# A hybrid decoder step on one core: the order of keys, queries, tables and sample work in the GLA heads, and of the couples' combinations

## The chip, the cores and the metric

One core of one Trainium2 chip. The metric is the device time of one execution in microseconds (us), the median of several runs. The kernel before ran three times: 1547.67 us median, 1545.2 to 1551.61.

## What is computed

One layer for a prompt of 2048 tokens and for eight single sample tokens, all float32, with a model width of 1024:

```python
ada = jax.nn.silu(c) @ w_ada + b_ada
shift, scale, gate = jnp.split(ada, 3, axis=-1)
hn = _rmsnorm(x, g_norm) * (1.0 + scale[:, None]) + shift[:, None]
z = hn @ w_in
xa, za, q, k, v, glr, zg = jnp.split(z, SPLITS, axis=-1)
...
log_alpha = jax.nn.log_sigmoid((glr @ w_gla_g2 + b_gla_g2).astype(f32)) / GLA_TAU
...
o, S_new = _gla_chunked(qh, kh, vh, log_alpha, S0.astype(f32))
o = o * lax.rsqrt(jnp.mean(o * o, axis=-1, keepdims=True) + EPS) * g_gla_norm.astype(f32)
y_gla = o.reshape(Bn, T, D_GLA).astype(x.dtype) * jax.nn.silu(zg)
mix = jnp.concatenate([y_lru, y_gla], axis=-1) @ w_out
x = x + gate[:, None] * mix
```

The first two columns of z, 1024 each, feed an RG-LRU group (convolution, gates, a real-gated recurrence, y_lru); the rest a gated linear attention (GLA) of four heads with keys of 128 and values of 256, whose decay comes from a product of rank 16 and a log-sigmoid. A last RMSNorm ends it.

## The kernel before

**Stages.** The prompt is worked in two halves of 1024 tokens. The stages follow one another on TensorE (PE): the adaLN vectors and the first head (0 to 90 us of the profile), the GLA heads of half 0 (to 366), the "couples" of half 0 (to 645; the RG-LRU's blocks and the columns of zg, each a 2x2 block product by seven products of a Strassen kind), the heads of half 1 (to 976), the couples of half 1 (to 1195), the output projection (to 1551). Every float32 operand of a product is split into a high and a low part, and each product is three products of these parts; splitting is a copy on ScalarE (ACT) and a subtraction on VectorE (DVE).

**Order.** ACT, DVE, GpSimd (POOL), the DMA queue of SyncE (SP) and PE each run their instructions strictly in the order in which they were written or scheduled, so a late instruction holds all that stand behind it. The order is written by a list of work that is due: `after(units, fn)` puts a piece of work into it, and `tick` lets it out when so many units of product work have been written. A unit is 24 products of 512 columns. `in_order`, `behind` and `issue_after` fix an engine's order where the scheduler might change it.

**A GLA head** (`gla_head`, L1107 and on) writes the value projection (`values`, eight tiles of 128 tokens, evicted at L893/894), and then for each segment s of 512 tokens: the decay (`decay`: product L913, ACT's L918, L920 exponential and L921 logarithm, DVE's L919 and L922; `gla_decay`: four scans L935, L944 exponential, L945, and L947/948 exponentials), the key projection (`project`, L683 to L685, 24 products; combined with the decay at L956) and the query projection (combined at L960). The chunks of the segment follow as due work: `gla_start` (scores L985, turned keys L988, their masks and splits L989 to L995), `gla_chunk` (L1011 to L1024, the state S at L1020), `gla_norm` (L1032), and one unit later `gla_turn`, which turns the normalized output on PE (L1080) for L1146 or, in the last head, for the gate at L1153. Exponential and logarithm are reached in ACT by loading a table set ahead of each use (the ACT_TABLE_LOAD rows of L920/921, L944 and L972); `silu` (L1084) uses a tanh. In half 1 the states of the sample tokens (`sample_state`, L795 to L809, L1043 to L1052) are worked between.

**Weights.** In half 0 weights are loaded raw (L332), split (L338 ACT, L339 DVE) and stored in DRAM (L365, `parts`); in half 1 they are loaded back (L341). `sample_cols` (products L302, copy L303, L308, L310) multiplies the eight sample tokens by the raw weight columns while they are there; in the first couples these products use the tiles called gps.

**Between the heads and the couples of half 0** `second_rows` normalizes the second 1024 rows of x (L242), turns them (L253) and adds them up on POOL for the Strassen operands; `sums` makes S1 to S4. `load_op` (L1202) brings S3 and S4 back by SP's queue and `split_op` (L1209/1210) splits them. `Couple.prepare` (L1359 to L1396) splits a couple's four weight blocks (L1368 ACT, L1369 DVE), runs the sample columns and combines the blocks on POOL (L1384 to L1386); T2 is the block that needs L1385. `acc` tiles, of which there are four banks of PSUM, take the products of projections, values, decays and couples; `tp` tiles (two banks) take turned tiles.

Of the kernel before, what the change touches and what calls it, by code (L numbers as in the profile page):

```python
# [37 lines left out]
CTS = (0, 8)  # L38
B11, T2, T1, B21, T3, B22, T4 = range(7)
# [13 lines left out]
def hybrid_kernel(ctx, tc, i, o):  # L53
# [243 lines left out]
    def sample_cols(raw, n, dst, tmp, bank, units=0.5):  # L297

        ps = bank()
        for r in range(2):  # L300
            for g in range(4):
                PE.matmul(ps[32 * g:32 * g + 32, :n], fs[:, 4 * r + g], raw(4 * r + g), start=r == 0, stop=r == 1)  # L302
        S.copy(tmp[:, :n], ps[:, :n])  # L303

        def turn():
            po = bank()
            for a in range(n // P):
                PE.matmul(po[:, a * NS:(a + 1) * NS], tmp[:, a * P:(a + 1) * P], sel4, start=True, stop=True)  # L308
            for a, (d, scale) in enumerate(dst):
                V.tensor_scalar(d, po[:, a * NS:(a + 1) * NS], scale, None, op0=OP.mult)  # L310
        after(units, turn)
# [42 lines left out]
    def raw_rows(col, n, k0=0, nk=KT):  # L354
        raw = wp.tile([P, 1088], F32, tag="wr", name="wr")[:, :nk * n].rearrange("p (k n) -> p k n", n=n)
        SP.dma_start(raw, i["w_in"][0, k0 * P:(k0 + nk) * P, col:col + n].rearrange("(k p) n -> p k n", p=P))
        return raw

# [228 lines left out]
    def first_head():  # L587
# [71 lines left out]
        with tc.issue_after(last[V.engine]), tc.issue_after(last[S.engine]):  # L659
            normalize(st, [xsr], NS, "junk")  # L660
# [248 lines left out]

    def decay(h, c0, n):  # L910
# [9 lines left out]
        S.activation(e, e, AF.Exp, scale=-1.0)  # L920
# [136 lines left out]
    def sample_out(h, b0, st, s0, done, more):  # L1057
# [13 lines left out]
        rsqrt(gp, rs[:, :1], ss[:, :1], 1, P, 1.0 / DV)  # L1071
        V.tensor_scalar(os_, os_, rs[:, :1], None, op0=OP.mult)
# [10 lines left out]
    def silu(z, src):  # L1083
        S.activation(z, src, AF.Tanh, scale=0.5)  # L1084
        V.scalar_tensor_tensor(z, z, 1.0, src, op0=OP.add, op1=OP.mult)
# [21 lines left out]
    def gla_head(half, h, k, wv=None, w=None):  # L1107
        final = k == 3
        if wv:
            wk, wq = wkq0  # L1110
            v, prep0, rest = first_head()
        else:
            v = values(half, h, w or value_weights(h))
            own = own_samples(half, h)
            wk = weights(K0 + h * DK, DK, samples=own)
            wq = weights(Q0 + h * DK, DK, samples=own)
            if own:
                after(1, lambda: sample_qk(h, 1, wk))
                after(2, lambda: sample_qk(h, 0, wq))
# [3 lines left out]
        def chunks(s, c):  # L1123
# [13 lines left out]
            after(1, lambda: finish(s), True)  # L1137
# [31 lines left out]
        for s in range(2):  # L1169
            if wv and s == 0:  # L1170
                prep[s] = prep0
                pk = project(wk, 512, 512)
                rest()
            else:
                prep[s] = gla_qk(h, s, wq, wk, dec, pk)
                pk = None
            if s == 0:
                dec = gla_decay(half, h, 1)
                after(0, lambda: chunks(0, 0), True)
            tick(0.5)  # L1180
        if half == 1 and k == 0:
            sample_heads(0)
        if wv:
            modulate_samples(st, xsr)
            with tc.issue_after(last[V.engine]), tc.issue_after(last[S.engine]):
                constants()
        if final:
            wz = [weights(ZG + (2 * h + dt) * P, P) for dt in range(2)]
            z = [gp.tile([P, 2, 512], F32, tag=tag, name="z", bufs=2) for tag in ("vh", "vl")]
            for dt in range(2):  # L1190
                for s in range(2):
# [5 lines left out]
                    tick(0.5)  # L1197

# [13 lines left out]
    def second_rows(sc, then):  # L1212
# [8 lines left out]
        def norm(p, x):  # L1221
            normalize(xp, x)
            after(0.5, lambda: step(p, x, 0))

        def step(p, x, k):
# [14 lines left out]
            elif p < 3:  # L1240
                after(0.5, lambda: load(p + 1))
            else:
                after(1.5, then)
# [12 lines left out]
    def sums(pool, then):  # L1256
# [20 lines left out]
        def other(k, s2):  # L1277
# [9 lines left out]
            after(*((1, lambda: one(k + 1)) if k < 3 else (1.5, then)))  # L1287
# [40 lines left out]
    class Couple:  # L1328
# [30 lines left out]
        def prepare(self, q):  # L1359
# [13 lines left out]
            if q == B11:  # L1373
                self.slot(q)
                split(q, b11)
                if self.half == 0:
                    tmp = am.rearrange("p c t -> p (c t)")
                    if turns[3]:
                        turns[3] = 0
                        tmp = lp.tile([P, 512 + 4], F32, tag="xa", name="tmp")  # L1380
# [4 lines left out]
                G.tensor_tensor(t, b22, b11, op=OP.subtract)  # L1385
                G.tensor_tensor(b12, b22, b12, op=OP.subtract)  # L1386
# [11 lines left out]
        keep = None  # L1398
# [262 lines left out]
    def couples(cs, lead=5, at={}):  # L1661

        n = len(cs)
        for k in (1, 2):
            cs[-k].turn = k
        uses = [(0, 0), (0, 1)]
# [9 lines left out]
        def prepare(u):  # L1676
            if u < len(uses):
# [3 lines left out]
                cs[m].prepare(q)  # L1681

        cs[0].load_raw()
        for u in range(lead):
            prepare(u)
# [12 lines left out]

    for k, h in enumerate(HEADS):
        gla_head(0, h, k, wv0 if k == 0 else None)  # L1700
# [32 lines left out]
    def samples_silu():  # L1733
        with behind(V), behind(S):
# [5 lines left out]
    scs.append(Scratch(3))  # L1740
    for k, h in enumerate(HEADS):
        gla_head(1, h, k, w=w if k == 0 else None)
# [543 lines left out]
```

## Time and profile before

| | |
|---|---|
| median of three runs | 1547.67 us |
| the profiled execution | 1552.06 us |
| its span in the profile | 1550.3 us |
| mean granted clock of PE | 0.971 |
| instructions | 22539 |

The profile is one execution. The page's first part gives each engine's busy time and share of the span. The windows give, for a stretch of time, its length and each engine's busy time with its count of instructions, then PE's granted clock (1.00 is full speed), the DMA engines' busy share and GB/s. The waits of an engine are its idle times, grouped by the instruction that waited and by the one that ended last before it could start ("PE tp L1080 <- DVE on L1032: 18.8, 5, 6.3" reads: PE's line 1080, which writes the tile tp, waited five times, 18.8 us in all and 6.3 us at most, and DVE's line 1032, which wrote the tile on, had ended last). The timeline has the start, the length, engine, line, operation, tiles out and in, sizes and count. In groups by line stand the count, busy time and the mean of one in ns, and after the bar the idle time before them. PE's products overlap, so a mean of 390 ns for 512 columns is longer than the distance between two starts.

### The profile page before, as it was taken

Reading aid. Unit: us, or ns where it says so; the run is one execution under the profiler, and the core shown is the slowest. Engines: PE = TensorE matmul, PEld = TensorE weight load, DVE = VectorE, ACT = ScalarE, POOL = GpSimd, SP = SyncE. Lnnn points to the kernel's source line nnn. Section 1 sums busy time; section 2 is a strip of 40 time slices with the busy share of each in tenths; the row PEclk is TensorE's granted clock in tenths of the full one; section 3 lists DMA queues with packets and bytes.
Section 4 is the critical chain, followed back from the end, with each engine's and each line's share of the span. In section 5 each row is a group of like instructions: output and inputs, shape, how many; then the busy total and the mean of one; then the engine's idle time right before and its main releaser. Section 6 shows DMA issues by size and latency. Waiting matters only on the chain.

```text
span 1550.3 us, 22539 instructions
## 1 busy us (share of the span) xinstructions
PE 1437.3 (93%) x8113; PEld 1185.5 (76%) x8113; DVE 1112.8 (72%) x2283; ACT 760.3 (49%) x1367; POOL 292.9 (19%) x285
## 2 busy tenths in 40 slices
PE   8979889899899999988887999999999699999997
PEld 6868778787677777878776788788888587778886
DVE  5775666466587888758786765576798597678886
ACT  4534445644665766444635351466775342144332
POOL 1450521224212222054253300000112000000000
PEclk9989999999999999999998999999999899999999
DMA  9625446646738644977866642876617848694452
GB/s 324 240 82 184 163 147 197 219 150 219 263 131 304 220 156 134 313 252 250 293 229 222 210 163 79 312 222 192 191 54 236 330 172 305 233 346 144 151 167 109
DMA packets 204293, 321.97 MB, mean 208 GB/s; under 512 B 11730, under 2 KB 145522, under 8 KB 200461
## 3 DMA queue, kind: packets, MB, share of 16 engines
q1 hardware_dynamic: 160133, 293.00, 55.4%
q10 hardware_dynamic: 43728, 26.48, 5.4%
q8 instruction: 64, 1.05, 0.3%
q0 software_dynamic: 320, 1.05, 0.2%
q14 instruction: 48, 0.39, 0.1%
HBM read 196.86 MB, written 123.68 MB: 207 GB/s over the span
## 4 chain that ended last, share of the span: by engine, by line
PE 55%; DVE 20%; DMA 11%; ACT 8%; issue 4%; POOL 1%; SPq 0%; ACTq 0%; DVEq 0%; POOLq 0%
PE acc L1914 11%; PE tp L1914 8%; PE acc L1415 8%; PE tp L1415 6%; PE acc L685 2%; PE acc L684 2%; PE acc L683 2%; PE acc L375 2%; PE acc L377 2%; PE acc L376 2%; DVE xb L935 2%; DMA mixd<-zs 1%; DVE tg L1556 1%; DVE op L1369 1%; PE po L1019 1%
## 5 line engine op out<-in xcount | busy, mean ns | idle before, releaser
L1415 PE MATMUL acc<-op,op 128*128 128x512 f32 x1056 | 252.5, 393 | 4.9 <-DVE op L1369 2.2
L1415 PEld LDWEIGHTS acc<-op,op 128*128 128x128 f32 x1056 | 199.8, 190 | 49.1 <-DVE op L1369 3.4
L1415 PE MATMUL tp<-op,op 128*128 128x512 f32 x792 | 199.2, 396 | 2.2 <-DVE acc L1425 2.1
L1914 PE MATMUL acc<-w,a 128*128 128x512 f32 (+1 forms) x792 | 187.9, 390 | 11.9 <-ACT a L1765 7.9
L1914 PEld LDWEIGHTS acc<-w,a 128*128 128x128 f32 x792 | 147.7, 190 | 47.7 <-ACT a L1765 8.8
L1415 PEld LDWEIGHTS tp<-op,op 128*128 128x128 f32 x792 | 147.6, 189 | 37.5 <-issue 4.1
L375 PE MATMUL acc<-w,op 128*128 128x256 f32 (+1 forms) x508 | 151.7, 299 | 1.0 <-DVE xb L960 1.0
L377 PE MATMUL acc<-w,op 128*128 128x256 f32 (+1 forms) x508 | 145.5, 286 | 1.5 <-DVE op L269 1.5
L376 PE MATMUL acc<-w,op 128*128 128x256 f32 (+1 forms) x508 | 144.9, 285 | 0.0
L1914 PE MATMUL tp<-w,a 128*128 128x512 f32 x564 | 136.0, 391 | 0.0
L683 PE MATMUL acc<-op,w 128*128 128x512 f32 x296 | 124.8, 422 | 3.0 <-DMA w<-parts 3.0
L1914 PEld LDWEIGHTS tp<-w,a 128*128 128x128 f32 x564 | 105.3, 188 | 26.8 <-issue 5.2
L684 PE MATMUL acc<-op,w 128*128 128x512 f32 x296 | 118.7, 401 | 0.0
L685 PE MATMUL acc<-op,w 128*128 128x512 f32 x296 | 118.6, 401 | 0.0
L375 PEld LDWEIGHTS acc<-w,op 128*128 128x128 f32 x508 | 97.9, 193 | 3.4 <-DVE xb L960 1.3
L377 PEld LDWEIGHTS acc<-w,op 128*128 128x128 f32 x508 | 97.7, 192 | 2.0 <-DVE op L269 1.9
L376 PEld LDWEIGHTS acc<-w,op 128*128 128x128 f32 x508 | 97.5, 192 | 0.7
L1384 POOL TENSOR_TENSOR raw<-raw 128x512 f32<-128x512 f32 x14 | 24.4, 1746 | 316.6 <-DVE op L1369 267.6
L1765 ACT CAST a<-s 128x512 fp32r<-128x512 f32 x61 | 36.4, 619 | 97.1 <-issue 34.3
L1523 DVE SCALAR_TENSOR_TENSOR cv<-xa,vecT,cv 128x512 f32<-128x512 f32 x96 | 73.3, 764 | 8.0 <-ACT cv L1521 6.9
L226 ACT ACTIVATE junk<-on 128x256 bf16<-128x256 f32 x64 | 26.6, 415 | 104.3 <-DVE on L1024 92.1
L683 PEld LDWEIGHTS acc<-op,w 128*128 128x128 f32 x296 | 57.0, 192 | 15.5 <-DMA w<-parts 3.7
(413 smaller groups left out, 2985.4 us busy)
## 6 DMA issues: line engine op xcount, KB each, us to landing
wtd<-op SPq DMA_DIRECT2D x56, 512.0 KB
op<-wtd SPq DMA_DIRECT2D x56, 512.0 KB
w<-parts SPq DMA_DIRECT2D x16, 1024.0 KB
a<-mixd SPq DMA_DIRECT2D x63, 256.0 KB
parts<-w SPq DMA_DIRECT2D x15, 1024.0 KB
mixd<-zs ACTq DMA_DIRECT2D x52, 256.0 KB
wd<-scratch SPq DMA_DIRECT2D x48, 256.0 KB
w<-wd SPq DMA_DIRECT2D x10, 1024.0 KB
```

The costliest lines, as they stand in the source:

```text
L226: S.activation(junk[:m, :n], x, AF.Square, accum_out=out)
L375: PE.matmul(ps, part(0, kt, c), hi[:, kt % 4], start=kt == 0, stop=False)
L376: PE.matmul(ps, part(0, kt, c), lo[:, kt % 4], start=False, stop=False)
L377: PE.matmul(ps, part(1, kt, c), hi[:, kt % 4], start=False, stop=kt == KT - 1)
L683: PE.matmul(ps[:, :n], hi[:, kt], a, start=kt == 0, stop=False)
L684: PE.matmul(ps[:, :n], hi[:, kt], b, start=False, stop=False)
L685: PE.matmul(ps[:, :n], lo[:, kt], a, start=False, stop=kt == KT - 1)
L935: V.tensor_tensor_scan(b3[:, c], b3[:, c], b3[:, c], 0.0, op0=OP.add, op1=OP.bypass)
L1415: PE.matmul(ps, w[:, u, k], t[:, v, k], start=q < 3 and (k, u, v) == (0, 0, 0), stop=(k, u) == (3, 1), skip_group_check=True)
L1523: V.scalar_tensor_tensor(cv, xa[:, k:k + 512], cw[k], cv, op0=OP.mult, op1=OP.add)
L1765: S.copy(t[:, 0, k], (low(t) if src is None else src)[:, k])
L1914: PE.matmul(ps, t[:, u, k], w[:, v, k, c], start=(q < 3 or ps is own) and (k, u, v) == (0, 0, 0), stop=(k, u) == (3, 1), skip_group_check= ...
```

## The change

It moves work, and hardly adds or removes any. By the built programs, PE, DVE and POOL run as many products and operations as before, SP's queue as many DMAs, and ACT 36 instructions fewer, all of them table loads on balance.

- In heads that aren't the first, the two key projections come first and then the two query projections (K0, K1, Q0, Q1; in the last head of each half K0, Q0, K1, Q1 as before), and the second segment's decay product is written right after the first key projection.
- A single table set that holds exponential and logarithm is loaded once by hand (`tables`), and again only after a tanh has needed the other one.
- Chunk work starts one unit after the keys and queries are ready (was: at once); turned outputs come two units after the norm (was one; only the last segment of the last head keeps one).
- Weights of the next head's values, of keys and of queries are loaded and split at written-out units (`ahead`, `take`), one head ahead for the values; the store follows half a unit later.
- Norm and scale of the second rows are split into two pieces; `sums` goes on half a unit earlier; in the couples the sample columns and POOL's combinations come 0.75 unit later (0.5 behind a zg couple), in steps of the same size; the samples' output scale and the norm of the first samples come later.

```diff
-    def sample_cols(raw, n, dst, tmp, bank, units=0.5):
+    def sample_cols(raw, n, dst, tmp, bank, units=1):
...
+    def take(col, n, k0, nk, raw):
...
+        if raw is None:
+            SP.dma_start(both[:, :, c].bitcast(F32), parts[col, k0])
+        else:
+            with behind(S), behind(V):
+                S.copy(hi, raw)
+                V.tensor_tensor(lo, raw, hi.bitcast(F32), op=OP.subtract)
...
+            after(0.5, lambda: SP.dma_start(parts[col, k0], both[:, :, c].bitcast(F32)))
...
+        if log_exp[0]:
+            return
+        log_exp[0] = True
+        with behind(S):
+            S.add_instruction(mybir.InstLoadActFuncSet(
+                name=nc.get_next_instruction_name(), engine=S.engine, act_func_set_id=LOG_EXP))
...
-            after(1, lambda: finish(s), True)
+            after(1 if final and s else 2, lambda: finish(s), True)
...
+            V.tensor_tensor(e2, pk, e2, op=OP.mult)
+            tick(0.5)
+            b = decay(h, *SEGS[1])
+            if not final:
+                pk = project(wk, *SEGS[1])
+                tick(0.5)
+            pq = project(got[1], *SEGS[0])
+            V.scalar_tensor_tensor(e1, pq, DK ** -0.5, e1, op0=OP.mult, op1=OP.mult)
+            prep[0] = e1, e2, f
+            after(1, lambda: chunks(0, 0), True)
+            tick(0.5)
+            if final:
+                pk = project(wk, *SEGS[1])
+                tick(0.5)
+            pq = project(got[1], *SEGS[1])
+            e1, e2, f = gla_decay(half, h, 1, b=b)
+            V.tensor_tensor(e2, pk, e2, op=OP.mult)
+            V.scalar_tensor_tensor(e1, pq, DK ** -0.5, e1, op0=OP.mult, op1=OP.mult)
...
         def norm(p, x):
-            normalize(xp, x)
-            after(0.5, lambda: step(p, x, 0))
+            with behind(S):
+                ss = squares(xp, x)
+            after(0.5, lambda: scale(p, x, ss))
...
+                times(x, scales(xp, ss, 2))
+            after(1, lambda: step(p, x, 0))
...
-            after(*((1, lambda: one(k + 1)) if k < 3 else (1.5, then)))
+            after(*((0.5, lambda: one(k + 1)) if k < 3 else (1.5, then)))
...
-                if self.half == 0:
...
-                    sample_cols(lambda kt: r[:, kt].rearrange("p b n -> p (b n)"), 2 * P,
-                                [(zsam[:, n], 1.0) for n in self.sam], tmp, gps)
-                t = self.t2 = lp.tile([P, 4, P], F32, tag="t2", name="t2")
-                G.tensor_tensor(b11, b12, b11, op=OP.subtract)
...
+                (self.combine if now else lambda: after(self.wait, self.combine))()
...
+        keep, wait = None, 0.75
```

Three places in the built order show what moves. Lines on the left are those of each kernel. The first is ACT in half 1, in the second head, where keys and queries are made. Before (e and xb are the decay's tiles, f its chunk ends, scratch the samples' states, smp the samples' decay):

```order
L920 ACTIVATE e<-e 128x512
L921 ACT_TABLE_LOAD
L921 ACTIVATE e<-e 128x512
L795 CAST scratch<-scratch 128x256
L944 ACT_TABLE_LOAD
L944 ACTIVATE f<-f 128x5
L947 ACTIVATE e<-xb 128x512
L918 ACTIVATE e<-acc,vecT 128x8
L948 ACTIVATE xb<-xb 128x512
L920 ACTIVATE e<-e 128x8
L921 ACT_TABLE_LOAD
L921 ACTIVATE e<-e 128x8
```

And now (ob is a turned output of the head before, L1222):

```order
L951 ACTIVATE e<-e 128x512
L952 ACTIVATE e<-e 128x512
L813 CAST scratch<-scratch 128x256
L975 ACTIVATE f<-f 128x5
L813 CAST scratch<-scratch 128x256
L978 ACTIVATE e<-xb 128x512
L947 ACTIVATE e<-acc,vecT 128x8
L979 ACTIVATE xb<-xb 128x512
L951 ACTIVATE e<-e 128x8
L952 ACTIVATE e<-e 128x8
L1222 ACTIVATE ob<-tp,gsc 128x512
L1003 ACTIVATE smp<-xb 128x8
```

The exponential (now L951) and logarithm (L952) stand without a load between them, as do L975, L978 and L979, and the turned output of the head before has come in among them.

The second is PE in the same head, from the second decay's product to the scores. Before (op and w are the operands of the projection, tp<-xb,e the scores, acc<-gls,g2s the decay):

```order
L913 MATMUL acc<-gls,g2s 128x512
L683 MATMUL acc<-op_6279,w 128x512
L684 MATMUL acc<-op_6279,w 128x512
L685 MATMUL acc<-op_6279,w 128x512
L683 MATMUL acc<-op_6279,w 128x512
L985 MATMUL tp<-xb,e 128x128 x4
L988 MATMUL tp<-ident,e 128x128 x4
```

And now, where the scores are L1016:

```order
L701 MATMUL acc<-op_6280,w 128x512
L702 MATMUL acc<-op_6280,w 128x512
L703 MATMUL acc<-op_6280,w 128x512
L701 MATMUL acc<-op_6280,w 128x512
L702 MATMUL acc<-op_6280,w 128x512
L703 MATMUL acc<-op_6280,w 128x512
L1016 MATMUL tp<-xb,e 128x128 x4
L1019 MATMUL tp<-ident,e 128x128 x4
```

The second decay's product, L913 before, stands four products ahead of the scores; now (L942) it stands 60 projection products ahead of them, with the turned outputs of the head before and two pieces of sample work between.

The third is PE early in the couples of half 0. Before (gps<-raw,fs are the first couple's next sample columns, gps<-sel_110,am the sum of their copies):

```order
L1415 MATMUL tp<-op_4013,op 128x512 x12
L1415 MATMUL tp<-op_1186,op 128x512 x7
L302 MATMUL gps<-raw,fs 32x256 x8
L1415 MATMUL tp<-op_1186,op 128x512 x3
L308 MATMUL gps<-sel_110,am 128x8 x2
L1415 MATMUL tp<-op_1186,op 128x512 x2
```

And now (L303 and L309 are these two, L1525 the couples' products, L1648 to L1650 the gates'):

```order
L303 MATMUL gps<-raw,fs 32x256 x8
L1525 MATMUL acc<-op_1185,op 128x512 x9
L1525 MATMUL acc<-op_147,op 128x512 x4
L1648 MATMUL gps<-xh,amh 128x512
L1525 MATMUL acc<-op_4122,op 128x512
L1649 MATMUL gps<-xl,amh 128x512
L1650 MATMUL gps<-xh,amh 128x512
L1648 MATMUL gps<-xh,amh 128x512
L1649 MATMUL gps<-xl,amh 128x512
L1650 MATMUL gps<-xh,amh 128x512
L1525 MATMUL acc<-op_4122,op 128x512 x11
L309 MATMUL gps<-sel_110,am 128x8 x2
```

The sum of the copies stood three products behind the columns; now it stands 25 products of the couples behind them. The columns themselves stand 20 products of the couples later than before.

More of the change, by code (lines that the diff above doesn't have):

```diff
@@ L38 @@
 CTS = (0, 8)
+LOG_EXP = 6
 B11, T2, T1, B21, T3, B22, T4 = range(7)
@@ L357, in raw_rows, with ahead @@
         return raw
+    def ahead(col, n, k0=0, nk=KT):
+        return None if (col, k0) in parts else raw_rows(col, n, k0, nk)
+    def take(col, n, k0, nk, raw):
+        q = 48 if n == DV else 0
+        c = slice(q, q + nk * n)
+        both = wp.tile([P, 2, 1088], F32R, tag="w", name="w", bufs=3)
+        hi, lo = [both[:, j, c].rearrange("p (k n) -> p k n", n=n) for j in range(2)]
+        if raw is None:
[4 more added lines that the diff above has]
+                V.tensor_tensor(lo, raw, hi.bitcast(F32), op=OP.subtract)
+            parts[col, k0] = dpool.tile([P, 2, nk * n], F32, tag=f"w{col}_{k0}", name="parts")
+            after(0.5, lambda: SP.dma_start(parts[col, k0], both[:, :, c].bitcast(F32)))
+        return [hi, lo, raw]
     def split_parts(n=2):
@@ L1168, in gla_head @@
             dec = gla_decay(half, h, 0)
[L1169 to L1179, printed above, removed]
-            tick(0.5)
+        if wv:
+            prep[0] = prep0
+            pk = project(wk, 512, 512)
+            rest()
+            b = decay(h, *SEGS[1])
+            after(1, lambda: chunks(0, 0), True)
+            tick(0.5)
+            prep[1] = gla_qk(h, 1, wq, wk, gla_decay(half, h, 1, b=b), pk)
+        else:
+            e1, e2, f = dec
+            if pk is None:
+                pk = project(wk, *SEGS[0])
+            V.tensor_tensor(e2, pk, e2, op=OP.mult)
+            tick(0.5)
+            b = decay(h, *SEGS[1])
+            if not final:
+                pk = project(wk, *SEGS[1])
[3 more added lines that the diff above has]
+            prep[0] = e1, e2, f
+            after(1, lambda: chunks(0, 0), True)
+            tick(0.5)
[6 more added lines that the diff above has]
+            V.scalar_tensor_tensor(e1, pq, DK ** -0.5, e1, op0=OP.mult, op1=OP.mult)
+            prep[1] = e1, e2, f
+        tick(0.5)
         if half == 1 and k == 0:
@@ L1183, in gla_head @@
         if wv:
+            with tc.issue_after(last[V.engine]), tc.issue_after(last[S.engine]):
+                normalize(st, [xsr], NS, "junk")
             modulate_samples(st, xsr)
@@ L1240, in step @@
             elif p < 3:
-                after(0.5, lambda: load(p + 1))
+                load(p + 1)
             else:
@@ L1396, in prepare, with combine @@
                 split(q, {B21: b21, T3: b12, B22: b22, T4: b11}[q])
-        keep = None
+        def combine(self):
+            r = self.raw
+            b11, b12, b21, b22 = [r[:, 4 * k:4 * k + 4, b] for k in range(2) for b in range(2)]
+            if self.half == 0:
+                tmp = am.rearrange("p c t -> p (c t)")
+                if turns[3]:
+                    turns[3] = 0
+                    tmp = lp.tile([P, 512 + 4], F32, tag="xa", name="tmp")
+                sample_cols(lambda kt: r[:, kt].rearrange("p b n -> p (b n)"), 2 * P,
+                            [(zsam[:, n], 1.0) for n in self.sam], tmp, gps, self.wait)
+            t = self.t2 = lp.tile([P, 4, P], F32, tag="t2", name="t2")
+            G.tensor_tensor(b11, b12, b11, op=OP.subtract)
+            G.tensor_tensor(t, b22, b11, op=OP.subtract)
+            G.tensor_tensor(b12, b22, b12, op=OP.subtract)
+        keep, wait = None, 0.75
         def begin(self):
@@ L1665, in couples @@
             cs[-k].turn = k
+        for c, prev in zip(cs[1:], cs):
+            if isinstance(prev, Zg):
+                c.wait = 0.5
         uses = [(0, 0), (0, 1)]
```

83 lines of the change are left out of this document (61 added, 22 removed).

## The prediction

> **What bounds the kernel now.** I read the page first, then the windows by stage, then the waits of TensorE, then the places of the waits in the windows and the timeline. The first columns of the windows are the stretch, its length and PE's busy time; PEclk is the first of the last three.
>
> ```profile
> PE 1437.3 (93%) x8113; PEld 1185.5 (76%) x8113; DVE 1112.8 (72%) x2283; ACT 760.3 (49%) x1367; POOL 292.9 (19%) x285
> ```
>
> ```profile
> 90.00:366.00 276.00, 252.87 (x1875) 218.51 (x1879) 171.31 (x469) 130.66 (x265) 69.46 (x91) 0.95 0.50 165
> 366.00:645.00 279.00, 262.35 (x1254) 205.49 (x1247) 224.56 (x327) 178.08 (x273) 68.25 (x45) 0.98 0.63 218
> 645.00:976.00 331.00, 297.79 (x1902) 258.60 (x1901) 222.71 (x633) 143.69 (x307) 96.87 (x98) 0.96 0.65 217
> 976.00:1195.00 219.00, 215.14 (x961) 175.77 (x960) 163.44 (x233) 140.02 (x214) 22.30 (x12) 1.00 0.61 191
> ```
>
> PE is the bound: 93% busy, and no other engine is near. The change leaves its products as they are, so it can only win what PE loses. Of the four stretches (heads of half 0, couples of half 0, heads of half 1, couples of half 1) three have something to give. PE stands idle 276 − 252.87 = 23.1, 279 − 262.35 = 16.7 and 331 − 297.79 = 33.2 us there, 73.0 in all, and a clock of 0.95, 0.98 and 0.96 costs about 0.05 × 276 + 0.02 × 279 + 0.04 × 331 = 32.6 us more: 0.45 us for each us of idle time. The last couples have 3.9 us and a full clock. The idle time by what ended it (total, times, longest):
>
> ```profile
> PE tp L1080 <- DVE on L1032: 18.8, 5, 6.3
> PE tp L985 <- DVE xb L960: 6.9, 4, 3.2
> PE pkv L1011 <- DVE S L1020: 6.4, 6, 2.2
> PE acc L913 <- DVE gls L850: 6.2, 1, 6.2
> PE po L1017 <- DVE aml L992: 6.1, 4, 3.1
> PE gps L302 <- DMA raw<-in_w_in_dram: 4.6, 3, 2.8
> PE gps L308 <- ACT am L303: 4.5, 6, 1.1
> PE gps L1538 <- DVE zsam L310: 4.0, 2, 2.0
> PE po L1015 <- DVE on L1024: 3.5, 2, 3.0
> PE tp L253 <- DVE scratch L242: 3.4, 5, 2.1
> PE tp L985 <- ACT e L920: 3.0, 1, 3.0
> PE acc L683 <- DMA w<-parts: 3.0, 2, 2.5
> ```
>
> These are 70.4 us, most of them in the three stretches. Every one is a short chain on DVE, ACT or a queue that is asked for too early in the program: the engines have the time, but not at that moment. That is what the change works on.
>
> That a wait costs more than its length is seen in the windows around three of them: the stretch of a wait of 1.96 us at 717.3, the stretch behind it, and stretches behind waits of 2.99 (at 758.3) and 2.48 us:
>
> ```profile
> 717.30:719.25 1.95, 0.00 (x1) 0.03 (x1) 1.84 (x7) 0.00 (x0) 1.12 (x2) 1.00 0.51 200
> 719.40:722.80 3.40, 3.40 (x16) 3.13 (x16) 2.17 (x7) 1.88 (x5) 0.00 (x0) 0.50 0.25 85
> 761.32:767.20 5.88, 5.88 (x22) 5.40 (x23) 4.19 (x10) 4.58 (x6) 0.00 (x0) 0.50 0.72 246
> 835.45:838.80 3.35, 3.35 (x9) 2.60 (x9) 2.61 (x11) 1.59 (x5) 2.53 (x2) 0.50 0.69 220
> ```
>
> Behind each, PE runs 3.4 to 5.9 us at half clock, which loses 1.7 to 2.9 us: a wait of 1.96 us was enough. I take the 0.45 per us of the stages. The Trainium skill ("TensorE: Matmul & The Clock Gate", Part 1, the HAM clock gate) lets the half rate come only after at least one idle window of about 3.4 us. The rows above speak against that as a threshold on the wait; what it would make of the sum is a rival below.
>
> **The change part by part.** The unit of delay is 24 products of 512 columns. From starts in the timeline of PE, (757.94 − 757.25) / 3 = 0.23 us a product, so a unit is 5.5 us and half a unit 2.8:
>
> ```profile
> 757.25 0.39 PE L683 MATMUL acc<-op,w 128*128 128x512 f32 x1
> 757.94 0.40 PE L683 MATMUL acc<-op,w 128*128 128x512 f32 x1
> 761.32 2.05 PE L985 MATMUL tp<-xb,e 128*128 128x128 f32 x8 [2.99 <-ACT e L920]
> ```
>
> *Turned outputs (L1080)* come one unit later. Waits of at most 6.3 us move by 5.5 us: 0.8 us stays of the longest, nothing of an average one (18.8 / 5 = 3.8). I count −17. DVE's norm itself is no shorter; it lies beside the extra 24 products.
>
> *Keys first, one table set (L985).* PE reaches the scores' products only four products after the second decay's product. On ACT, in that wait:
>
> ```profile
> 754.92 0.20 ACT L920 ACTIVATE e<-e 128x8 f32<-128x8 f32 x1
> 755.13 1.28 ACT L921 ACT_TABLE_LOAD   x1
> 756.42 0.21 ACT L921 ACTIVATE e<-e 128x8 f32<-128x8 f32 x1
> 758.36 1.70 ACT L1051 ACTIVATE scratch<-scratch,smp 128x256 f32<-128x256 f32 x4
> 760.66 0.63 ACT L920 ACTIVATE e<-e 128x512 f32<-128x512 f32 x1
> ```
>
> ```profile
> L921 ACT ACT_TABLE_LOAD x20 | 25.7, 1283 | 0.4
> L944 ACT ACT_TABLE_LOAD x16 | 20.5, 1283 | 0.7 <-ACT scratch L1229 0.4
> ```
>
> DVE's queue stands behind L1051's samples, and L1051 behind loads of 1.28 us. The order has 36 loads fewer: 36 × 1.283 = 46 us of ACT's time. None is worth its length to PE, since ACT is half idle; what counts is two or three of them inside one chain, about 2.6 to 3.8 us. In the new order about 60 products (13.8 us) lie between the second decay's product and the scores. The chain they have to cover, for one segment of 512 tokens:
>
> ```profile
> L935 DVE TENSOR_TENSOR_SCAN xb<-xb 128x128 f32<-128x128 f32 x64 | 31.2, 546 | 0.2
> L945 DVE TENSOR_TENSOR xb<-xb,mid 128x512 f32<-128x512 f32 x16 | 13.5, 844 | 0.3
> L956 DVE TENSOR_TENSOR e<-acc,e 128x512 f32<-128x512 f32 x15 | 10.4, 690 | 10.0 <-ACT e L947 4.5 <-PE acc L685 4.4 <-ACT scratch L1051 1.1
> L960 DVE SCALAR_TENSOR_TENSOR xb<-acc,xb 128x512 f32<-128x512 f32 x16 | 11.0, 687 | 11.6 <-PE acc L685 11.6
> ```
>
> 4 × 0.55 + 0.84 + 0.69 + 0.69 = 4.4 us of DVE, and ACT's part between. It fits in 13.8 even for two segments. Of 6.9 + 3.0 I count −8.5; if that cover failed, the 9.9 would all stay.
>
> *Sample columns of the first couples.* Their products and the copies they wait for come 0.75 unit (4.1 us) later and half as dense. The three rows sum to 13.1; each single wait is at most 2.8. Three quarters go: −10, since the raw columns' DMA isn't earlier.
>
> *Weights later.* Splits, stores and loads go out at set units, and the loads from parts up to a head earlier: −2.5 of 3.0. In the first head the split below stood between PE and the cast that its wait of 6.2 us names:
>
> ```profile
> 83.31 2.27 DVE L339 TENSOR_TENSOR w<-wr,w 128x1024 fp32r<-128x1024 f32 x1
> 90.64 0.67 DVE L850 CAST gls<-tp 48x512 fp32r<-48x512 f32 x1
> ```
>
> It is gone from there: −2.3; the samples' norm, small operations in the same queue, mostly stays. One product of chunks later (L1015) gives about −1.2 more: −3.5.
>
> *Norm of the second rows split in two* (L253): −2 of 3.4. *Chunk products a unit later*: the waits for S and aml (6.4 + 6.1) depend on DVE's queue at that moment, which gets no shorter: anything from 0 to −12; I take −3, by the few table loads that no longer stand ahead of them.
>
> Sum of waits: −(17 + 8.5 + 10 + 2.5 + 3.5 + 2 + 3) = −46.5; with 0.45 of clock each, −67.
>
> **Given back.** No row shows the new waits. Two prices. The second rows now end later, and with them the load and split of the operand S3, which the order puts behind raw loads and stores of the couples' operands on SP's queue:
>
> ```profile
> 365.53 0.33 SPq L1202 DMA_DIRECT2D op<-sd  x1
> 387.32 0.89 SPq L1202 DMA_DIRECT2D op<-sd  x1
> ```
>
> The first went out at 365.5, at the couples' start; it may slip about 6 us or more, and PE stands for what its cover of three products of 12 doesn't hide: between 0 and 11, I take 5. And the products of keys, scores and chunks meet other work at their new places: I expect six new waits of the average size of L985's now (6.9 / 4 = 1.7), with clock 6 × 1.7 × 1.45 = 15; bounds 0 and 40 (fourteen segments, 2 us each, with clock). Net: −67 + 5 + 15 = −47. The profiled execution took 1552.06 us, 4.4 more than the median of the runs, 1547.67: so 1505 for such an execution, and 1500 for a median. A measurement of this kernel can tell about 0.5%, 7.7 us, from no change.
>
> **Rivals.** *DVE late in the heads of half 1.* It is busy 222.71 of 331 us there, with states of samples among it; if the moved chains queue behind those, half of the gain comes back: about 1524. For it: most waits above name DVE. Against it: the new distance of 13.8 us. Chance 0.15.
>
> *Clock not won.* If only waits as long as such a stretch, 3.4 us, bring half clock, and the shorter ones met it for another reason, then of the waits that go four or so count (L1080's longest, the first head's), at 1.7 to 2.9 us each: about 9 us of clock instead of 21, so 1512. The stretch behind 1.96 us speaks against it. Chance 0.05. This is the rule of the Trainium skill's page on TensorE, cited above.
>
> *Nothing but moved waits.* By the order the loads are gone and the products moved, so the change does what it says; yet all gaps could reopen one step on, since ACT and DVE are slack on average only: 1548. Chance 0.07.
>
> *Slower: accumulator banks.* There are four. The second keys now stay in one until the second decay's chain is done, which before was drained first; the second queries take another. Two are left, that is about one unit, 5.5 us, of further products. The chain is 4.4 us of DVE and some 1 us of ACT: just covered. It decides from the point where DVE has more than that queued ahead. If 7 us a head were queued uncovered, in the seven heads with this order, 7 × 7 × 1.45 = 71 us come back: 1571. Against it: in the order the second keys' operation mostly stands ahead of or next to the first queries'. Chance 0.08.
>
> **How the numbers follow.** The forecast has the other 0.65. Its own range: all of it and the chunks' other 9 (× 1.45) with nothing given back is 1500 − 20 − 13 = 1467; with 40 + 11 given back it is 1531. The range of 1470 to 1532 holds it and the first two rivals, about 0.82. Faster 0.65 + 0.15 + 0.05 = 0.85, same 0.07, slower 0.08.
>
> **What would show it.** Right: L1080's row below 3 us, L985's two below 2, the gps rows below 4; the clock 0.97 or more in the heads' stages; no loads at the decay's lines. Wrong: rows of 5 us and more at S3's split, at the scores' operands or at PE's acc of keys and values, or waits gone with the clock as before. The couples of half 1 and the output projection should stay within 2 us.

## The result and the profile after

The changed kernel took 1532.3 us (median of 4 runs, 1530.7 to 1535.28) against 1547.12 for the kernel before (4 runs): a ratio of 0.9902, interval 0.9875 to 0.9929. It is faster by 15 us, a third of the 47 that were forecast, and lies just outside the range. The profiled execution of the changed kernel has a span of 1531.5 us.

The page after has the same PE work and less idle time: the idle part of the span was 1550.3 − 1437.3 = 113.0 us and is 94.4.

```profile
span 1531.5 us, 22483 instructions
...
PE 1437.1 (94%) x8113; PEld 1186.1 (77%) x8113; DVE 1102.8 (72%) x2283; ACT 714.5 (47%) x1331; POOL 292.2 (19%) x285
```

The windows of the three middle stages (heads of half 0, couples of half 0, heads of half 1), cut at the first product of the second decay, the first and the last product of the couples of half 0 and the first of those of half 1. The kernel before, cut so:

```profile
91.40:366.50 275.10, 253.34 (x1880) 218.57 (x1880) 170.41 (x468) 130.73 (x266) 69.46 (x91) 0.95 0.50 164
366.50:642.50 276.00, 259.35 (x1227) 202.95 (x1224) 222.07 (x325) 177.41 (x272) 68.25 (x45) 0.98 0.63 218
642.50:964.10 321.60, 288.39 (x1868) 251.20 (x1866) 219.51 (x630) 140.39 (x302) 96.87 (x98) 0.96 0.65 215
```

And the changed kernel:

```profile
90.30:362.10 271.80, 254.22 (x1880) 219.12 (x1880) 173.37 (x471) 115.19 (x253) 68.42 (x88) 0.96 0.51 169
362.10:641.70 279.60, 260.87 (x1225) 203.06 (x1224) 227.54 (x323) 178.43 (x273) 74.35 (x49) 0.98 0.63 219
641.70:945.30 303.60, 281.80 (x1868) 247.51 (x1867) 203.15 (x629) 113.43 (x282) 93.09 (x98) 0.98 0.69 225
```

So the heads of half 0 gained 3, the couples of half 0 lost 4, and the heads of half 1 gained 18. The waits of PE, those that answer to the rows of before and the new ones:

```profile
PE gps L309 <- ACT tx L1651: 7.3, 6, 1.9
PE acc L942 <- DVE gls L868: 6.2, 2, 4.4
...
PE tp L309 <- DVE mixs L311: 4.6, 1, 4.6
PE po L1046 <- DVE on L1055: 4.4, 2, 2.7
PE po L1046 <- DVE os L1098: 3.0, 1, 3.0
PE tp L309 <- ACT ob L1222: 2.9, 2, 2.5
PE tp L309 <- ACT tmp L304: 2.7, 1, 2.7
...
PE gps L309 <- ACT am L304: 2.4, 1, 2.4
...
PE gps L1648 <- ACT am L304: 2.1, 3, 1.2
PE acc L701 <- ACT w L373: 1.9, 1, 1.9
...
PE po L1048 <- DVE aml L1023: 1.7, 2, 0.9
...
PE gps L303 <- DMA raw<-in_w_in_dram: 1.6, 1, 1.6
PE acc L701 <- DMA w<-parts: 1.6, 1, 1.6
...
PE tp L1016 <- DVE xb L991: 1.4, 1, 1.4
PE tp L1115 <- ACT ob L1222: 1.3, 1, 1.3
...
PE tp L254 <- DVE scratch L243: 0.9, 3, 0.5
```

The rows that were aimed at did fall: turned outputs (L1080, now L1115) from 18.8 to 1.3, scores from 9.9 to about 1.7, the second rows' turn from 3.4 to 0.9. In their place stand waits for L309, the sum of the sample columns: 7.3 + 4.6 + 2.9 + 2.7 + 2.4 = 19.9 us. The 2.7 and the 2.4 are waits for the copies that are summed (L304), as were the 5.4 us of the same sums (L308) before. The other 14.8 us are new, and they are waits for a bank of PSUM to write, of two kinds, tp and gps. The sums used the same banks before: what the change moved is their time, not their place. How one of these waits arises is seen in the timeline of the first half's second head, DVE first and then PE:

```profile
155.16 5.44 DVE L966 TENSOR_TENSOR_SCAN xb<-xb 128x128 f32<-128x128 f32 x4
...
162.53 0.16 DVE L311 TENSOR_SCALAR mixs<-tp 128x8 f32<-128x8 f32 x1
...
162.83 0.57 PE L309 MATMUL tp<-sel,tmp 128*128 128x8 f32 x2 [4.60 <-DVE mixs L311]
```

The sum of the queries' columns needs a tp bank; the one that it gets holds the sum of the keys' columns, whose reader, a 0.16 us copy on DVE (L311), stands behind four scans. In the couples it is the same with the two gps banks, which the gates' products use as well and which ACT's L1651 frees behind a scan:

```profile
423.55 2.28 DVE L1666 TENSOR_TENSOR_SCAN tg<-a,tx 128x1024 f32<-128x1024 f32 x1
...
425.87 0.69 ACT L1651 ACTIVATE tx<-gps,hbx 128x512 f32<-128x512 f32 x1 [2.49 <-DVE tg L1666]
...
426.61 0.61 PE L309 MATMUL gps<-sel,am 128*128 128x8 f32 x4 [1.82 <-ACT tx L1651]
```

That is a reading of one execution. The experiments ask what each part is worth.

### The profile page after: what moved, and what is told of

Same layout as the page of the kernel before. It is cut to its first block, busy times and chain, and to the rows that moved or that the text cites. A ratio compares the mean times of both kernels' runs of the same rounds, so it can differ in the third digit from the quotient of the medians.

```text
span 1531.5 us, 22483 instructions
## 1 busy us (share of the span) xinstructions
PE 1437.1 (94%) x8113; PEld 1186.1 (77%) x8113; DVE 1102.8 (72%) x2283; ACT 714.5 (47%) x1331; POOL 292.2 (19%) x285
## 4 chain that ended last, share of the span: by engine, by line
PE 59%; DVE 18%; DMA 11%; ACT 6%; issue 4%; POOL 2%; SPq 1%; ACTq 0%; DVEq 0%; POOLq 0%
PE acc L2030 11%; PE acc L1525 8%; PE tp L2030 8%; PE tp L1525 7%; DMA wd<-scratch 4%; PE acc L396 3%; PE acc L397 3%; PE acc L395 2%; PE acc L701 2%; PE acc L702 2%; PE acc L703 2%; DVE tg L1666 2%; PE po L1050 1%; DVE cv L1633 1%; DMA op<-fd 1%
## 5 line engine op out<-in xcount | busy, mean ns | idle before, releaser
L1525 PE MATMUL acc<-op,op 128*128 128x512 f32 x1056 | 256.8, 397 | 5.6 <-DMA op<-wtd 2.6
L1525 PEld LDWEIGHTS acc<-op,op 128*128 128x128 f32 x1056 | 200.1, 191 | 50.2 <-ACT op L1308 4.3
L1525 PE MATMUL tp<-op,op 128*128 128x512 f32 x792 | 198.0, 396 | 2.1 <-DVE acc L1535 2.1
L1525 PEld LDWEIGHTS tp<-op,op 128*128 128x128 f32 x792 | 149.3, 191 | 35.1 <-DVE acc L1535 2.5
L1051 DVE TENSOR_TENSOR S<-S,pkv 128x256 f32<-128x256 f32 x60 | 25.1, 418 | 70.2 <-PE po L1050 69.5
```

The lines of the kernel that those rows point to most:

```text
L1525: PE.matmul(ps, w[:, u, k], t[:, v, k], start=q < 3 and (k, u, v) == (0, 0, 0), stop=(k, u) == (3, 1), skip_group_check=True)
```

## The experiments

Each was timed beside the kernel before on the same chip; the ratio is to that kernel's runs there. The stages are those of the windows above, in one profiled execution of each, which is not always a typical one: it took 6 us more than the median for the table set in the old order and 4 more for the loads at the logarithm, but 7 less for the kernels with 17 loads and with loads aside and 10 less for the late turned outputs in the old order. Where the text gives a part's worth, it is by the medians and ratios, if it names no stage.

| kernel | median us | ratio | interval | heads 0 | couples 0 | heads 1 |
|---|---|---|---|---|---|---|
| before | 1547.1 | 1 | | 275.1 | 276.0 | 321.6 |
| changed | 1532.3 | 0.9902 | 0.9875 to 0.9929 | 271.8 | 279.6 | 303.6 |
| changed, couples' part undone | 1530.5 | 0.9884 | 0.9859 to 0.9908 | 274.7 | 272.4 | 306.0 |
| changed, turned outputs early | 1532.7 | 0.9905 | 0.9883 to 0.9926 | 268.5 | 283.0 | 307.7 |
| changed, K0 Q0 K1 Q1 | 1538.7 | 0.9951 | 0.9932 to 0.9969 | 271.4 | 279.2 | 310.3 |
| changed, without the table set | 1550.1 | 1.0013 | 0.9995 to 1.0031 | 281.3 | 278.3 | 313.7 |
| before + table set | 1528.4 | 0.9875 | 0.9852 to 0.9897 | 265.4 | 273.3 | 313.0 |
| changed, heads' sums on acc | 1527.8 | 0.9871 | 0.9846 to 0.9895 | 259.1 | 278.8 | 309.3 |
| changed, couples' sums on acc | 1538.3 | 0.9929 | 0.9907 to 0.9951 | 278.5 | 276.0 | 305.5 |
| changed, couples undone, heads' sums on acc | 1521.7 | 0.9821 | 0.9800 to 0.9841 | 261.8 | 271.8 | 307.5 |
| before + table set + 17 loads at the exponential | 1528.1 | 0.9860 | 0.9837 to 0.9883 | 259.7 | 272.1 | 310.6 |
| before + table set + loads aside (19 more) | 1532.7 | 0.9893 | 0.9867 to 0.9919 | 263.5 | 271.9 | 311.6 |
| couples undone, sums on acc, turned outputs early | 1527.0 | 0.9862 | 0.9841 to 0.9883 | 267.6 | 272.5 | 311.4 |
| before + table set + turned outputs late | 1521.8 | 0.9837 | 0.9813 to 0.9861 | 255.5 | 272.6 | 304.3 |
| before + table set + planned loads at both places | 1536.5 | 0.9942 | 0.9920 to 0.9963 | 260.0 | 275.3 | 319.5 |
| before + table set + planned loads at the logarithm | 1539.6 | 0.9958 | 0.9936 to 0.9979 | 264.0 | 273.8 | 326.4 |

**The parts, one undone at a time.** First the couples:

```diff
-                (self.combine if now else lambda: after(self.wait, self.combine))()
+                self.combine()
...
-                            [(zsam[:, n], 1.0) for n in self.sam], tmp, gps, self.wait)
+                            [(zsam[:, n], 1.0) for n in self.sam], tmp, gps, 0.5)
```

> The changed kernel with the couples' part undone: sample columns and combinations at once behind the first block's split, their sum 0.5 unit later, as before. Theory (the waits of the sample columns were not removed but moved onto the two banks that the gates' products use and that ACT frees late): the couples of half 0 fall from 279.6 us to about 276, the whole from 1532 to about 1528. Rival (the part saved its 10 us and something else ate them): the couples grow by some 10 us and the whole is about 1542.

Measured 1530.5, and the couples of half 0 at 272.4 in place of 279.6. The stage says what the theory said: this part made the couples slower by about 7 us, not faster by 10. The whole moved by 2 us only, which its interval doesn't tell from nothing. Its waits: none for the gates' bank at L309, but some 3.7 for raw columns as before.

```profile
PE gps L1648 <- DVE zsam L311: 5.7, 4, 2.0
...
PE gps L303 <- DMA raw<-in_w_in_dram: 3.7, 3, 2.0
...
PE gps L309 <- ACT am L304: 3.0, 4, 1.1
```

Then the turned outputs:

```diff
-            after(1 if final and s else 2, lambda: finish(s), True)
+            after(1, lambda: finish(s), True)
```

> The changed kernel with the turned outputs one unit after the norm again. Theory (this term of the prediction was right, and its waits alone were worth 17 us and some clock): 1547 to 1556, with PE's wait for the norm back at 15 us or more. Rival (the other moves already give DVE its time, so the later turn is worth little): below 1538.

Measured 1532.7: no difference. The theory that this term was right fell. With the old delay in the new order PE waits for the norm 7.8 us, not 15 or more, and the time is the same:

```profile
PE tp L1115 <- DVE on L1063: 7.8, 8, 2.7
```

The order of keys and queries:

```diff
-            if not final:
+            if False:
                 pk = project(wk, *SEGS[1])
...
-            if final:
+            if True:
                 pk = project(wk, *SEGS[1])
```

> The changed kernel with K0, Q0, K1, Q1 in every head, the rest as changed (the second decay still right behind the first keys, chunks a unit later). Theory (the later chunks and the shorter chain on ACT, not the order of keys and queries, took the waits at the scores away): within 4 us of 1532. Rival (keys first is what covers the second decay): 1540 or more, with waits at the scores of 6 us or more.

Measured 1538.7, some 6 us slower than the change as a whole, with intervals that are just disjoint; the waits at the scores come back to 2.9 + 2.0 + 1.7 = 6.6 us.

```profile
PE po L1050 <- DVE S L1052: 4.9, 2, 4.6
...
PE pkv L1042 <- DVE S L1051: 3.8, 3, 1.4
...
PE tp L1016 <- DVE mixs L311: 2.9, 1, 2.9
...
PE tp L1016 <- DVE xb L991: 2.0, 1, 2.0
...
PE tp L1016 <- DVE xb L1264: 1.7, 1, 1.7
```

The end result lies between the two expectations and nearer to the rival, so keys first is worth its place. That it is worth it by covering the second decay is shown in part only: the 2.9 is a wait for a tp bank that still holds a sample sum, and more than at the scores comes back at the state S in the chunks, 4.9 + 3.8 us where the changed kernel has 0.8. The table set:

```diff
-        if log_exp[0]:
-            return
-        log_exp[0] = True
+        return
```

> The changed kernel without the one table set: exponential and logarithm load a set each time again, some 42 loads of 1.28 us more on ACT. Theory (ACT has the time, and the chains are covered now): 1532 to 1537. Rival (ACT's loads sit in the chains that PE waits for): 1545 or more, so that the tables alone are the whole gain.

Measured 1550.1, a ratio of 1.0013: the rival, and clearly. Without the table set the whole new order is worth nothing. ACT's loads are back, 36 more than in the changed kernel:

```profile
L950 ACT ACT_TABLE_LOAD x20 | 25.7, 1283 | 0.4
...
L973 ACT ACT_TABLE_LOAD x15 | 19.2, 1283 | 1.0 <-ACT ob L1220 0.8
```

By stage the new order alone loses 6 us in the heads of half 0 (281.3 against 275.1) and 2 in the couples, and gains 8 in the heads of half 1 (313.7 against 321.6).

**The table set alone, and the banks.** The next four follow from that. The table set in the old order (the function `tables`, its call, and the three places that reset its flag, taken over unchanged):

```diff
-        S.activation(e, e, AF.Exp, scale=-1.0)
+        tables()
+        with behind(S):
+            S.activation(e, e, AF.Exp, scale=-1.0)
```

> The kernel before with the one table set alone: 36 loads fewer on ACT, all work in its old order. Without the table set the changed kernel was as slow as before. Theory (the loads in the chains are the gain and the new order is worth nothing): 1528 to 1536. Rival (the two need each other: the old order has the same waits whatever ACT does, and only the new one lets the shorter chains pay): 1541 or more.

Measured 1528.4 (0.9875): the theory. One part of the change, with next to nothing moved (in the traces, loads left aside, 5 of ACT's 1289 instructions and 7 of PE's 8113 are out of their old order), gives at least the whole gain. PE's waits show no single place where it came from; the rows of before are all still there, most of them somewhat lower (18.8, 9.9, 6.4 and 6.1 for these):

```profile
PE tp L1094 <- DVE on L1046: 16.5, 6, 6.3
...
PE tp L999 <- DVE xb L974: 5.6, 3, 2.9
PE pkv L1025 <- DVE S L1034: 4.0, 4, 2.2
...
PE po L1031 <- DVE aml L1006: 3.9, 3, 3.4
...
PE tp L999 <- ACT e L934: 2.3, 1, 2.3
```

Next, the banks. The heads' sample columns (keys, queries, zg) on the accumulators, `acc` for `tps`:

```diff
-        sample_cols(lambda kt: w[2][:, kt], P, [(qks[:, n, h], (DK ** -0.5, 1.0)[n])], tmp, tps)
+        sample_cols(lambda kt: w[2][:, kt], P, [(qks[:, n, h], (DK ** -0.5, 1.0)[n])], tmp, acc)
...
-                        sample_cols(lambda kt: wz[dt][2][:, kt], P, [(zsam[:, 2 * h + dt], 1.0)], tmp, tps)
+                        sample_cols(lambda kt: wz[dt][2][:, kt], P, [(zsam[:, 2 * h + dt], 1.0)], tmp, acc)
```

> The changed kernel with the sample columns of keys, queries and zg in the heads on the four accumulator banks in place of the two banks of turned tiles. Theory (their new waits, 10.2 us behind an eviction of a turned tile or behind the sums' own copy, come from these two banks): the waits go, about 1524. Rival (the accumulators are as full, the waits move to projections): 1530 or more.

Measured 1527.8: about half way, 5 us faster than the change by the ratios, though their intervals overlap. The heads of half 0 fell from 271.8 to 259.1 in the profiled executions, and of the 10.2 us that L309 waited there 0.3 are left, so these waits were the banks' doing; a new one of 6.0 us appeared at an accumulator that holds keys:

```profile
PE acc L701 <- DVE e L1257: 6.0, 1, 6.0
```

The couples' columns on the accumulators, `acc` for `gps`:

```diff
-                            [(zsam[:, n], 1.0) for n in self.sam], tmp, gps, self.wait)
+                            [(zsam[:, n], 1.0) for n in self.sam], tmp, acc, self.wait)
```

> The changed kernel with the couples' sample columns on the accumulator banks in place of the two banks that the gates' products use. Theory (these two banks, freed by ACT behind a scan of DVE, hold the sums up for 9.7 us): the couples of half 0 fall from 279.6 to about 273, the whole to about 1526. Rival (the couples' products hold the accumulators): the couples grow, 1535 or more.

Measured 1538.3: a miss by the theory, though the interval overlaps that of the changed kernel. The couples did fall, to 276.0, but the heads before them grew to 278.5 (the first columns, 16 products, are worked there now), and waits came up at the couples' own tp bank and at the first columns' data:

```profile
PE tp L1525 <- DVE acc L1535: 6.9, 3, 3.4
...
PE acc L303 <- DMA raw<-in_w_in_dram: 5.5, 1, 5.5
```

So the banks as the cause of the couples' loss are read from the timeline above and not shown by a run.

The couples' part undone and the heads' columns on the accumulators together:

> The changed kernel with the couples' part undone and the heads' sample columns on the accumulator banks. If both hold up PE independently: about 1522, the couples of half 0 at 272. If the time between the stages is made up elsewhere: 1528 to 1532.

Measured 1521.7, a ratio of 0.9821: the two at least add up, and this kernel beats both the one before and the changed one. Its interval lies clear of that of either repair alone (0.9859 to 0.9908 and 0.9846 to 0.9895). So each of the two repairs is a gain clear of noise where the other is made already: 9 us for the heads' sums, 6 for the couples' part.

**What a turned output and a load are worth.** The late turn again, in the repaired kernel and in the old order with the table set, where PE still waits 16.5 us for the norm (the diff of the second experiment above, the one way and the other):

> The kernel with the couples' part undone and the heads' sample columns on the accumulators (1521.7), with turned outputs one unit after the norm again. By the run that undid this part alone: no difference, 1518 to 1526. If the later turn pays once its new neighbours no longer wait for the same two banks: 1530 or more.

> The old order with the one table set (1528.4; PE still waits 16.5 us for the norm there) and turned outputs two units after the norm, alone. By the prediction's term of 17 us with its clock: 1504 to 1511. Rival (the time comes back at other places as it did in the new order): 1524 to 1530.

Measured 1527.0 (5 us more than 1521.7; the intervals 0.9841 to 0.9883 and 0.9800 to 0.9841 only touch) and 1521.8 (7 us less than 1528.4, by ratios 0.9837 against 0.9875, intervals overlapping). So in these two kernels the later turn is worth some 5 to 7 us, hardly clear of noise, and by no means 25. That it was worth nothing in the changed kernel because of the two shared banks is a guess: the runs don't tell 0 from 5 there, and in the old order the heads' sums use the same two banks. In the old order no wait for the norm is left in the trace, and the largest rows are the chunks' and the scores':

```profile
PE po L1031 <- DVE aml L1006: 7.1, 4, 2.9
PE tp L999 <- DVE xb L974: 6.9, 4, 2.3
```

The profiled execution of that kernel, 1511.9 us, was the quickest of its seven runs (up to 1526.3), so its stages flatter it. The table set and the late turn in the old order are as good as all of the new order repaired.

Then loads put back by hand into the old order with the table set, which the compiled kernel loads again even where the set is in place. Ahead of each decay's exponential:

```diff
-        if log_exp[0]:
-            return
-        log_exp[0] = True
```

> The old order with the one table set, which took 1528.4 against 1549.0, but with the load repeated ahead of the exponential in each decay: 17 loads (21.8 us of ACT) more, each inside the chain of a decay; half of what the set had saved. Theory (the gain is in the chains, in proportion): 1536 to 1541. Rival (one load in a chain is covered, only two in a row are late): 1532 or less.

And three units after each decay:

```diff
+        def aside():
+            log_exp[0] = False
+            tables()
+        after(3, aside)
```

> The same kernel with 21 loads more (26.9 us of ACT) in another place, three units after each decay, where ACT evicts values and squares outputs. Theory (only what stands in a decay's chain counts, ACT being idle half of the time): 1528 to 1532. Rival (every chain of short steps runs through ACT, and 1.28 us are late wherever they stand): 1538 to 1543.

Measured 1528.1 and 1532.7: 17 loads in the chain cost nothing, those elsewhere (19 more by the trace, not the 21 that were expected) 3 to 4 us, with intervals that overlap that of the kernel without them. So neither the number of loads in the chains nor ACT's time as such explains 20 us. But the loads of before differ from these in a second way: the order doesn't know of them. Taking 36 of them out moved 7 of PE's 8113 instructions, as was said above; the 17 written by hand moved 82 of them, and 43 of ACT's 1289, against the kernel without them. So, at the old places, by hand:

```diff
         with behind(S):
             S.activation(e, e, AF.Exp, scale=-1.0)
+        with behind(S):
+            S.add_instruction(mybir.InstLoadActFuncSet(
+                name=nc.get_next_instruction_name(), engine=S.engine, act_func_set_id=LOG_EXP))
```

and the same three lines ahead of the chunk ends' exponential.

> The old order's kernel with the one table set, and a load written by hand at each of the places where the kernel before had one (ahead of the logarithm, ahead of the chunk ends' exponential): 78 loads as before, but known when the order is planned, so that it moves about 1 in 16 of ACT's rows and 1 in 20 of PE's. Theory (time in the chains is what costs): 1544 to 1550, as before. Rival (loads that the plan doesn't know of are what costs): 1528 to 1534.

> The same with the loads ahead of the logarithm alone, 20 of them, planned for. Theory (in proportion to the loads in the chain): 1538. Rival (planned loads cost nothing): 1528 to 1532. If only the second load of a decay is late: 1528 to 1532 here and 1545 with both.

Measured 1536.5 with both and 1539.6 with those at the logarithm alone; their intervals overlap, and both lie between the kernel with the set (0.9875) and the one before (1). Neither theory holds alone. The first kernel has as many loads as the one before:

```profile
L936 ACT ACT_TABLE_LOAD x20 | 25.7, 1283 | 0.3
L962 ACT ACT_TABLE_LOAD x16 | 20.5, 1283 | 0.3
```

and takes 9 us less, 0.9942 (0.9920 to 0.9963). It differs from it in three things that these runs don't tell apart: its order (156 of PE's instructions stand elsewhere), the places of the second kind of load, of which only 5 of 16 are still right ahead of the chunk ends' exponential (L964), and the set, which is in place already where the loads of before change it. In ACT's own rows the last makes no difference: 1283 ns and at most 0.02 us to the instructions on either side, in both. One of the loads that went astray:

```profile
750.47 1.28 ACT L962 ACT_TABLE_LOAD   x1
751.77 0.62 ACT L1011 CAST amh<-am 128x512 fp32r<-128x512 f32 x1
...
755.15 0.21 ACT L964 ACTIVATE f<-f 128x5 f32<-128x5 f32 x1 [2.27 <-DVE f L958]
```

The other 10 to 13 of the 20 us go with the load between exponential and logarithm: with it alone the scores' wait is 14.0 us, against 5.6 + 2.3 without, and the heads of half 1 take 319.5 and 326.4, near the 321.6 of before, against 313.0.

```profile
PE tp L1097 <- DVE on L1049: 17.5, 8, 6.3
PE tp L1002 <- DVE xb L977: 14.0, 7, 3.5
```

Why the same load one instruction earlier, ahead of the exponential, costs nothing is open: the orders of all these kernels differ in other rows too, and they were not taken apart. That the table set is the gain is shown; how 36 loads come to cost 20 us is shown in part only.

## Why the prediction was wrong

**The step that failed.** The rows of waits went as forecast, and the time did not. The prediction's twelve rows stood at 70.4 us and were to lose 46.5. Those that answer to them in the changed kernel sum to 20.5, a loss of 49.9. But PE's idle time as a whole fell by 18.6, from 113.0 to 94.4, so some 31 us of waits came up in other rows. "Given back" allowed for six new waits of 1.7 us, 10 us in all, and for 5 us at S3: half of what came. With the waits went their clock. It was to give 21 us, less 5 given back, and PE's busy time over the whole span fell by 0.2 (1437.3 to 1437.1). The experiments say which part of the sum held: without the table set the new order gains nothing, and the set alone makes the gain. So the terms for the order took waits that vanish from their rows for time that is won, and all together they won none.

**Table loads.** "None is worth its length to PE, since ACT is half idle; what counts is two or three of them inside one chain" put them into the term for the scores, 8.5 us with those. They were worth 20 by themselves, 0.44 of the 46 us of ACT's time that they took. This term alone makes the measured gain. It was priced at the one wait whose timeline showed the loads, while in the old order with the table set most rows of the waits are a little lower. Some 9 of the 20 us are gone when as many loads are written by hand; what makes these cheaper is open, as said above.

**Turned outputs.** "I count −17", which is 25 with clock. PE's row for them fell by 17.5, as forecast, and the time didn't follow: undoing the part changed nothing. At 5 to 7 us in the two other kernels, the term was too large by at least three times. In the changed kernel the sample sums stand close to the turned outputs and want the same two tp banks, as the waits of L309 for ob show; that this is where the gain went was not shown.

**Sample columns.** "Three quarters go: −10" had the wrong sign. The rows that it meant did fall, from 13.1 us to 4.0. But the question was asked of the data that the products wait for, and not of the banks that they write, which another instruction has to free first. The heads' sums, which the change moved against the turned outputs and the decays' scans, cost some 5 to 9 us in the whole, the couples' part 2 to 6 (7 in its stage).

**Scores.** −8.5: their waits fell by 8.2, and undoing the order of keys and queries costs 6.4 us. The size was about right, in part by luck, since more than half of what comes back then is at the state S and at a bank.

**Smaller terms.** Weights and the first head, −2.5 and −3.5, came only in part: the wait for parts fell from 3.0 to 1.6, with 1.9 new behind ACT's split, the first head's from 6.2 to 4.4, with 1.8 of the same kind in half 1, and L1015's row rose from 3.5 to 4.4. The chunks' waits for S and aml fell by 10.8, not by 3, and the second rows' by 2.5 for the 2 forecast.

**Clock.** "0.45 of clock each", 21 us for 46.5 us of waits. In the three stages, cut where PE changes work, idle time fell from 71.6 to 58.1 us and PE's busy time, in which products at half clock count longer, from 801.1 to 796.9: 4.2 us of clock for 13.5 of idle time, 0.31 each. The first stage and the couples of half 1 lost 2.0 us each, so that nothing is left over the span. The new waits bring their own stretches of half clock: the 3.4 us behind that of 4.60 us ran at a granted clock of 0.50, those behind that of 1.82 us at 0.60. These sums do not decide the threshold of the Trainium skill ("TensorE: Matmul & The Clock Gate", Part 1, the HAM clock gate), an idle window of about 3.4 us before the half rate; the stretch behind 1.82 us speaks against it as a threshold on the wait, as the prediction's rows did.

**S3.** Its split shows 0.9 and 1.3 us, less than the 5 forecast.

**The rivals.** By the number the nearest was DVE late in the heads of half 1, at 1524, and it was the wrong place: that stage gained 18 us, the most of the three, and the loss was in the couples of half 0. By the mechanism it was "Nothing but moved waits", at 1548: that is what the new order did without the table set, at 1550.1. Its chance was 0.07, and it took the missing loads for nothing too. The slower rival, of accumulators held by keys, didn't show in the changed kernel; it showed once, with 6.0 us, when the sums were put there too. For the stages that were to stay within 2 us the forecast nearly held: 252.3 for the couples of half 1 against 250.1, and 333.9 against 336.1 behind them. Of its signs of being right, those on L1080 and L985 and the loads came true, while the clock in the heads was 0.96 and 0.98 for "0.97 or more", and one gps row was at 7.3 for "below 4".

## What to carry to other kernels

A row of waits that falls to nothing is no gain until the same part undone makes the kernel slower: take the waits as a list of suspects, and time each part alone. When small work is moved away from data that comes late, look first at whose banks it will write and at which queue its last reader stands in. Table loads were cheap to remove here and cost more than the one wait in which they were seen; look whether the order of the program was made with them or without.

## What the hardware showed unexpectedly

A table load takes 1283 ns in every run, also when the set that it loads is in place already, and the instructions on either side follow within 0.02 us where they have nothing else to wait for. Four scans took 5.44 us in the timeline above, 1.36 each, where the 50 scans of this line during which POOL ran nothing took 0.41 on the average and at most 0.43. POOL ran 128x512 additions in nearly all of that time:

```profile
154.66 1.61 POOL L1359 TENSOR_TENSOR scratch<-scratch,op 128x512 f32<-128x512 f32 x1
...
160.40 1.26 POOL L1359 TENSOR_TENSOR scratch<-scratch,op 128x512 f32<-128x512 f32 x1
```

Of the other 14 scans of the line, the four above among them, which all had POOL at work beside them, 12 took 0.7 us and more. The two belong together in time, over the whole trace; that the one slows the other was not tried apart.
